# A hybrid decoder block on one core: fewer rotary temporaries, another order of the second block's projections, and a rearranged opening

## The chip, the cores and the metric

The kernel runs on one core of a Trainium2 chip, in one launch. The metric is the device time of that core in microseconds (us), the median of several runs. TensorE (PE in the profile) does the matrix products, VectorE (DVE), ScalarE (ACT) and GpSimd (POOL) the rest, and SyncE (SP) issues nearly all transfers.

## The reference

One layer of a decoder block, float32, 2048 tokens of width 1024 (`x`, one sequence), with a conditioning vector `c`:

```python
mod = c @ w_ada + b_ada
shift_m, scale_m, gate_m, shift_f, scale_f, gate_f = jnp.split(mod, 6, axis=-1)
h = rms_norm(x, g_pre_mix) * (1 + scale_m) + shift_m
q_a, k_a, v_a, q_m, k_m, v_m, o_m, i_m, f_m, g_a, g_m = jnp.split(h @ w_in, split_points, axis=-1)
q_a, k_a = rope(q_a, positions), rope(k_a, positions)      # 8 and 2 heads of 64
y_a = sliding_window_attention(q_a, k_a, v_a, attn_sinks)  # window 128, blocks of 128
qk_m = silu(causal_depthwise_conv([q_m, k_m], conv_w, conv_b))
y_m = sigmoid(o_m) * head_layer_norm(mlstm_chunkwise(q_m, k_m, v_m, i_m + b_i, f_m + b_f), mlstm_norm_w)
merged = sigmoid(g_a) * (y_a @ w_branch_attn) + sigmoid(g_m) * (y_m @ w_branch_mlstm)
x = x + gate_m * rms_norm(merged @ w_out, g_post_mix)
h2 = rms_norm(x, g_pre_ffn) * (1 + scale_f) + shift_f
x = x + gate_f * rms_norm((silu(h2 @ w_ffn_gate) * (h2 @ w_ffn_up)) @ w_ffn_down, g_post_ffn)
```

The mLSTM is a recurrence over time with 4 heads of 128, computed in chunks. `w_ada` is 1024 x 6144, `w_in` 1024 x 4872.

## The kernel before

**Products.** Every large product is done as three TensorE products of rounded high and low parts (`hi`, `lo`, in a 32-bit type for TensorE): for weights ACT makes `whi` (L256, L259) and DVE `wlo` (L257, L260); L204 is the line of all products, L209 that of all transposes. A group of products on one weight slice for four token tiles of 128 fills four PSUM banks, the accumulators `acc`; four more banks (`mix`) serve transposes, attention, the mLSTM and other small products.

**Stages.** The tokens are four blocks of 512, b0 to b3, and two superblocks of two blocks each. The stages with their times in the profile:

- The opening (0 to 66 us). Shift and scale are computed from `w_ada` in four chunks of 256 columns (`ADA`, `ada_first`): the 8 row groups of a chunk are multiplied by the matching element of `c` and summed on DVE (L426, L428), then columns are summed by a product with ones. The shift of the first chunk goes over TensorE: 8 products with `c` as the stationary operand, a copy of the row by ACT (L443), and products that turn it into columns. L448 to L450 make shift and scale columns of it. Between the chunks `hprep` makes the normalized, shifted and scaled, transposed h of b0: squares by ACT (L500), root on POOL (L475), scaling (L506), transposes, high part by ACT (L518), the full value by ACT (L520), low part (L521) by POOL for the first block and by DVE for the others. The products of q for b0 follow the two feature tiles of each chunk as they come.
- Projections of the first block of the superblock (b0, from 66 us; b2, from 750 us): q, kv (k, v and the mLSTM's i and f), vm (the mLSTM's v); then of the second block: vm, q, kv, to about 240 and 960 us. Attention of the first block runs between the second block's products.
- Fourteen pairs, each a product for both blocks of the superblock at once, in seven products instead of eight: mLSTM q and k (`qk`), o (`om`), the two gates (`ga`, `gm`). The mLSTM's chunks run beside them. Then the branch products and `w_out` for each block (`outputs`). To about 750 and 1300 us.
- The FFN (1300 us to the end).

**Rotary tiles.** A tile of q (128 tokens x 512) or k leaves its accumulator by an ACT copy into a buffer `raw` of the pool `tx` (L781 for q, L805 for kv). `rope` takes two more, `y` and `z`: y gets raw times cosine (L758), z the crossed products with sine (L759, L760), L761 and L762 put them together in y. Later, `q_stream` transposes y on TensorE and takes two more `tx` for the high and low parts, which SP stores to `at_d` (L773); `k_stream` takes one more. vm's tiles take one `tx` each (L827) and are stored. The pool `tx` has 9 buffers of 128 x 512; a buffer that is stored is free when its store has landed. `tx` also serves the weights of `ada_stream`, the running computation of the other shift, scale and gate columns, and temporaries of the pairs.

**Order.** The program is written as a list of pieces of TensorE work (`program`, `superblock`); generators (`spawn`) with due times in estimated nanoseconds of TensorE work put their next step between the pieces (`tick`), and `finish` runs a generator to its end. A scheduler then orders each engine's instructions by a model of the times; each engine works off its own queue in order. SP's queue holds nearly all transfers in the order in which they are issued, and a transfer that is issued waits for the landing of one issued some transfers before.

**mLSTM.** In `chunk_state` (L1001), for a chunk of 128 tokens and four heads, the decay weights are exp(min(nb + cl, cneg)): four DVE instructions of 128 x 128 (L1022) and one exp of 128 x 512 (L1023); 16 chunks.

Of the kernel before, what the change touches and what calls it, by code (L numbers as in the profile page):

```python
# [49 lines left out]
ADA = [(0, 256, (0,)), (256, 256, ()), (512, 256, ()), (768, 256, ())]  # L50
# [21 lines left out]
def decoder_block(ctx: ExitStack, tc: tile.TileContext, a: dict, out: bass.AP, dbg=None):  # L72
# [76 lines left out]
    posi = tm([S // P, P], I32)  # L149
    nc.sync.dma_start(posi, a["positions"].rearrange("o (t p) -> (o t) p", p=P))  # L150
    c_sb = const.tile([P, KD], F32, name="c_sb")
    nc.sync.dma_start(c_sb, a["c"].rearrange("o (p k) -> (o p) k", k=KD))
# [3 lines left out]
    nc.sync.dma_start(sinks, a["attn_sinks"].to_broadcast([P, HQ]))  # L156
    ada_raws = {c0: load_ada(c0, n) for c0, n, _ in ADA[:ADA_AHEAD[0]]}
# [272 lines left out]
    def ada_first(c0, n, raws, on_pe):  # L430

        t0, nt = c0 // P, n // P
        acc = [tm([P, n]) for _ in range(2)]
        pt = mix_tile()
        ps = {part: mix_tile() for part in on_pe}
        for k in range(KD):
            for part in (0, 1):
                if part in on_pe:
                    mm(ps[part][0:1, :n], c_sb[:, k:k + 1], raws[part][k], k == 0, k == KD - 1)
                else:  # L440
                    ada_terms(acc[part], raws[part][k].unsqueeze(1), k, 1)
        for part in on_pe:
            A.copy(acc[part][0:1, :], ps[part][0:1, :n])  # L443
        for part in (0, 1):
            r = 1 if part in on_pe else P
            for j in range(nt):
                mm(pt[:, part * 8 + j:part * 8 + j + 1], acc[part][:r, j * P:(j + 1) * P], ones[:r, 0:1], True, True)
        V.tensor_tensor(sh1[:, t0:t0 + nt], pt[:, :nt], col("b_ada", t0, nt), op=ALU.add)  # L448
        V.tensor_tensor(s1[:, t0:t0 + nt], pt[:, 8:8 + nt], b1[:, 8 + t0:8 + t0 + nt], op=ALU.add)
        V.tensor_tensor(s1[:, t0:t0 + nt], s1[:, t0:t0 + nt], col("g_pre_mix", t0, nt), op=ALU.mult)  # L450
# [35 lines left out]
    def hprep(b, first=False):  # L486
# [25 lines left out]
        def one(k):  # L512
# [8 lines left out]
            (G if first else V).tensor_tensor(lo, v, hi.bitcast(F32), op=ALU.subtract)  # L521
# [192 lines left out]

    hp0 = hprep(0, first=True)
    next(hp0)
    tables = {}
# [18 lines left out]
    def superblock(sb):  # L736
# [9 lines left out]
        def rope(raw, heads, b, t):  # L746
# [7 lines left out]
            y = tx([P, W])  # L754
# [1112 lines left out]
```

## Time and profile before

| | us |
|---|---|
| median of 3 runs | 2722.19 (2721.7 to 2723.53) |
| profiled execution | 2727.14 |
| its span | 2725.4 |
| TensorE busy | 2644.5 (97%) |
| DVE busy | 1999.1 (73%) |
| ACT busy | 1287.0 (47%) |
| POOL busy | 152.6 (6%) |

The profile is of one execution, 4.95 us above the median of the runs; 1.7 us lie outside its span. In its rows L12 is line 12 of the kernel, `out<-in` are the program's names with the buffer numbers left out, a number in square brackets is the idle time of the engine just before, with what ended it. A row of a group gives the count, then the total busy time in us, the mean ns of one, and the idle time before them. The clock (PEclk) is that granted to TensorE as a share of the full one. Shares of busy time are means over stages that differ; the windows by stage are read for what one stage is worth.

### The profile page before, as it was taken

How to read it: one execution, taken by the hardware profiler on the slowest of the kernel's cores; microseconds unless marked ns; L12 is line 12 of the kernel's file. 1: busy time of each engine (PE TensorE's matmuls, PEld its weight loads, DVE VectorE, ACT ScalarE, POOL GpSimd, SP SyncE). 2: the span in 40 equal slices, each digit the busy share in tenths (PEclk: the TensorE clock that was granted, in tenths of full speed). 3: DMA queues.
4: the chain of work that ended last, by engine and by line, in shares of the span. 5: the costliest groups of instructions: out<-in, count | busy, mean ns of one | idle time of the engine just before them, and what ended most of it. 6: DMA issues, size and time to landing. Idle time of an engine off the chain costs nothing.

```text
span 2725.4 us, 35775 instructions
## 1 busy us (share of the span) xinstructions
PE 2644.5 (97%) x12310; PEld 2136.0 (78%) x12310; DVE 1999.1 (73%) x3954; ACT 1287.0 (47%) x2510; POOL 152.6 (6%) x189
## 2 busy tenths in 40 slices
PE   6999999999989899999999999999999999999998
PEld 4767778888877677888887888888877888888886
DVE  7959877866786988876587777776677676766456
ACT  5555743444755564334563443335554333333444
POOL 2010101100101010110000000000000000000000
PEclk8999999999999999999999999999999999999999
DMA  7755445697675554568765664436675332324566
GB/s 248 234 154 179 147 136 168 206 333 255 219 231 187 177 160 153 180 218 315 255 198 199 198 192 155 147 121 213 204 272 194 102 115 86 112 93 147 185 210 216
DMA packets 353639, 511.89 MB, mean 188 GB/s; under 512 B 25121, under 2 KB 213661, under 8 KB 348209
## 3 DMA queue, kind: packets, MB, share of 16 engines
q1 hardware_dynamic: 353456, 509.61, 56.6%
q8 instruction: 97, 1.59, 0.2%
q14 instruction: 86, 0.70, 0.1%
HBM read 357.12 MB, written 144.02 MB: 184 GB/s over the span
## 4 chain that ended last, share of the span: by engine, by line
PE 77%; DVE 7%; issue 4%; DMA 2%; ACT 2%; POOL 0%; SPq 0%; DVEq 0%; POOLq 0%; ACTq 0%
PE acc L204 54%; PE mix L204 22%; DVE hl L1354 1%; PE mix L209 1%; ACT hl L1353 1%; DMA at_d<-tx 1%; DMA raw<-as_d 1%; DVE tx L1132 1%; DMA raw<-in_w_ffn_down_dram 1%; DMA raw<-ws_d 0%; DVE w L1664 0%; DVE big L1354 0%; DVE big L552 0%; POOL rs L475 0%; DMA x1n<-tm 0%
## 5 line engine op out<-in xcount | busy, mean ns | idle before, releaser
L204 PE MATMUL acc<-big,hl 128*128 128x512 f32 x3936 | 947.7, 394 | 13.7 <-ACT tx L805 5.9
L204 PEld LDWEIGHTS acc<-big,hl 128*128 128x128 f32 x3936 | 732.8, 189 | 183.3 <-issue 10.2
L1353 ACT CAST hl<-raw 128x512 fp32r<-128x512 f32 x732 | 439.4, 621 | 500.5 <-PE acc L204 233.0
L1354 DVE TENSOR_TENSOR hl<-raw,hl 128x512 fp32r<-128x512 f32 x732 | 495.8, 694 | 193.6 <-ACT hl L1353 192.6
L204 PE MATMUL acc<-whi,big 128*128 128x512 f32 (+1 forms) x1280 | 380.8, 378 | 19.0 <-ACT big L518 8.4
L204 PEld LDWEIGHTS acc<-whi,big 128*128 128x128 f32 x1280 | 236.4, 192 | 65.9 <-ACT big L518 8.5
L204 PE MATMUL mix<-big,hl 128*128 128x512 f32 x1056 | 263.9, 390 | 1.6 <-ACT hl L1353 1.0
L204 PE MATMUL acc<-wlo,big 128*128 128x512 f32 (+1 forms) x640 | 241.8, 380 | 3.4 <-DVE wlo L260 3.4
L204 PE MATMUL acc<-hl,hl 128*128 128x512 f32 x1008 | 237.0, 393 | 4.7 <-DVE hl L1354 2.9
L204 PEld LDWEIGHTS mix<-big,hl 128*128 128x128 f32 x1056 | 197.7, 188 | 46.0 <-DVE hl L1354 1.8
L204 PEld LDWEIGHTS acc<-hl,hl 128*128 128x128 f32 x1008 | 187.1, 188 | 49.8 <-DVE hl L1354 8.4
L204 PE MATMUL mix<-hl,hl 128*128 128x512 f32 x792 | 183.2, 391 | 2.3 <-ACT hl L1353 1.4
L204 PEld LDWEIGHTS mix<-hl,hl 128*128 128x128 f32 x792 | 147.7, 188 | 37.0 <-DVE hl L1354 3.3
L260 DVE TENSOR_TENSOR wlo<-raw,whi 128x1024 fp32r<-128x1024 f32 (+1 forms) x96 | 108.8, 1133 | 71.8 <-ACT whi L259 65.1
L259 ACT CAST whi<-raw 128x1024 fp32r<-128x1024 f32 (+1 forms) x96 | 94.5, 985 | 128.6 <-PE acc L204 123.2
L204 PE MATMUL acc<-big,whi 128*128 128x512 f32 x512 | 154.9, 391 | 0.0
L204 PEld LDWEIGHTS acc<-wlo,big 128*128 128x128 f32 x640 | 123.1, 192 | 29.6 <-DVE wlo L260 5.1
L475 POOL TENSOR_TENSOR rs<-ms,nhalf 128x1 f32<-128x1 f32 (+1 forms) x56 | 42.7, 774 | 1642.4 <-DVE ms L473 1639.7
L204 PE MATMUL mix<-hcT4h,hl 128*128 128x512 f32 x352 | 117.6, 394 | 0.7 <-ACT hl L1353 0.7
L204 PE MATMUL acc<-hcT2h,hl 128*128 128x512 f32 x352 | 117.5, 394 | 0.0
L204 PEld LDWEIGHTS acc<-big,whi 128*128 128x128 f32 x512 | 95.7, 188 | 19.6
L204 PE MATMUL acc<-big,wlo 128*128 128x512 f32 x256 | 96.3, 392 | 0.0
(331 smaller groups left out, 3482.3 us busy)
## 6 DMA issues: line engine op xcount, KB each, us to landing
raw<-in_w_in_dram SPq DMA_DIRECT2D x48, 1024.0 KB
as_d<-w SPq DMA_DIRECT2D x154, 256.0 KB
raw<-as_d SPq DMA_DIRECT2D x70, 512.0 KB
raw<-in_w_ffn_gate_dram SPq DMA_DIRECT2D x22, 1024.0 KB
raw<-in_w_ffn_up_dram SPq DMA_DIRECT2D x22, 1024.0 KB
raw<-ws_d SPq DMA_DIRECT2D x40, 512.0 KB
tx<-in_w_ada_dram SPq DMA_DIRECT2D x64, 256.0 KB
y_d<-tm SPq DMA_DIRECT2D x64, 256.0 KB
```

The costliest lines, as they stand in the source:

```text
L204: T.matmul(o, lhsT=lhsT, rhs=rhs, start=start, stop=stop, skip_group_check=resumed)
L209: T.transpose(o, i, ident[:k, :k])
L259: A.copy(hv, src)
L260: V.tensor_tensor(lv, src, hv.bitcast(F32), op=ALU.subtract)
L475: G.tensor_tensor(r[:, :n], ms[:, :n], nhalf[:, :n], op=ALU.pow)
L1132: V.scalar_tensor_tensor(ac, u[:, j:j + TB], col("conv_w", j * 8 + f), ac, op0=ALU.mult, op1=ALU.add)
L1353: A.copy(v(hi), src)
L1354: V.tensor_tensor(v(lo), src, v(hi).bitcast(F32), op=ALU.subtract)
```

## The change

1. Loads of the opening: x's first half and positions, `c`, the first chunk of `w_ada`, then x's second half; eight loads of small vectors are issued by ScalarE's queue instead of SP's.
2. Shift and scale of the first chunk and the shift of the second go over TensorE, now with a 128 x 128 piece of `w_ada` as the stationary operand and a column of `c` as the moving one, so that the result is a column: 48 products of one column in place of 8 products of 256 and the products that turned rows into columns; the ACT copy goes, and 16 DVE terms. Scale is finished by one DVE instruction a column instead of two for both.
3. The first block's low parts (L521, eight of them) go from POOL to DVE, and the first superblock's rotary tables are emitted ahead of the chunks instead of ahead of the fourth.
4. `rope` works in place in `raw` with one temporary `z`: two `tx` a tile. `q_stream` puts its high part into z and its low part into raw; `k_stream` puts its parts into z.
5. The second block of a superblock is projected in the order kv, q, vm instead of vm, q, kv.
6. The mixer's gate (`ada_stream`) starts at the fifth pair of the first superblock instead of behind b0's kv, with 6000 instead of 5000 ns between its steps. The first eight pairs are in another order; the last `qk` pair takes the place of the second `ga` pair ahead of the point at which the mLSTM starts.
7. `chunk_state` adds nb and cneg in one DVE instruction and leaves cl to the bias of four exps of 128 x 128.

The instructions that TensorE issues from the FFN's first products on keep their order.

```diff
-ADA = [(0, 256, (0,)), (256, 256, ()), (512, 256, ()), (768, 256, ())]
+ADA = [(0, 256, (0, 1)), (256, 256, (0,)), (512, 256, ()), (768, 256, ())]
...
-    x_first = [load_x(x_d, big, 0)]
-
     stack = tm([P, P])
     V.memset(stack, 0.0)
+    posi = tm([S // P, P], I32)
+    nc.sync.dma_start(posi, a["positions"].rearrange("o (t p) -> (o t) p", p=P))
+    x_first = [load_x(x_d, big, 0)]
+    c_sb = const.tile([P, KD], F32, name="c_sb")
+    nc.sync.dma_start(c_sb, a["c"].rearrange("o (p k) -> (o p) k", k=KD))
+    ada_raws = {c0: load_ada(c0, n) for c0, n, _ in ADA[:ADA_AHEAD[0]]}
+    x_first.append(load_x(x_d, big, 1))
...
-        nc.sync.dma_start(stack[r0:r0 + n, :], v)
+        nc.scalar.dma_start(stack[r0:r0 + n, :], v)
...
-    x_first.append(load_x(x_d, big, 1))
...
-    nc.sync.dma_start(b_if, a["b_if"].to_broadcast([P, 8]))
+    nc.scalar.dma_start(b_if, a["b_if"].to_broadcast([P, 8]))
...
-    ada_raws = {c0: load_ada(c0, n) for c0, n, _ in ADA[:ADA_AHEAD[0]]}
...
-        acc = [tm([P, n]) for _ in range(2)]
-        pt = mix_tile()
-        ps = {part: mix_tile() for part in on_pe}
+        acc = {part: tm([P, n]) for part in (0, 1) if part not in on_pe}
+        pt = mix_tile() if acc else None
+        cols_ = {(part, j): (mix_tile if acc else acc_tile)()[:, :1] for part in on_pe for j in range(nt)}
         for k in range(KD):
             for part in (0, 1):
                 if part in on_pe:
-                    mm(ps[part][0:1, :n], c_sb[:, k:k + 1], raws[part][k], k == 0, k == KD - 1)
+                    for j in range(nt):
+                        mm(cols_[part, j], raws[part][k][:, j * P:(j + 1) * P], c_sb[:, k:k + 1], k == 0, k == KD - 1)
                 else:
                     ada_terms(acc[part], raws[part][k].unsqueeze(1), k, 1)
-        for part in on_pe:
-            A.copy(acc[part][0:1, :], ps[part][0:1, :n])
...
-        V.tensor_tensor(s1[:, t0:t0 + nt], pt[:, 8:8 + nt], b1[:, 8 + t0:8 + t0 + nt], op=ALU.add)
-        V.tensor_tensor(s1[:, t0:t0 + nt], s1[:, t0:t0 + nt], col("g_pre_mix", t0, nt), op=ALU.mult)
+        for j in range(nt):
+            t = t0 + j
+            V.tensor_tensor(sh1[:, t:t + 1], cols_[0, j], col("b_ada", t), op=ALU.add)
+            V.scalar_tensor_tensor(s1[:, t:t + 1], cols_[1, j], b1[:, 8 + t:9 + t], col("g_pre_mix", t), op0=ALU.add, op1=ALU.mult)
...
-            (G if first else V).tensor_tensor(lo, v, hi.bitcast(F32), op=ALU.subtract)
+            V.tensor_tensor(lo, v, hi.bitcast(F32), op=ALU.subtract)
...
     hp0 = hprep(0, first=True)
     next(hp0)
-    tables = {}
+
+    tables[0] = rope_tables(0)
...
-            y = tx([P, W])
-            z = tx([P, W])
...
-            return y
+            z = tx([P, 512])
...
+            V.tensor_tensor(zz[:, :, 0, :], src[:, :, 1, :], sb_, op=ALU.mult)
+            V.tensor_tensor(zz[:, :, 1, :], src[:, :, 0, :], sb_, op=ALU.mult)
+            V.tensor_tensor(rr, rr, cb, op=ALU.mult)
+            V.tensor_tensor(src[:, :, 0, :], src[:, :, 0, :], zz[:, :, 0, :], op=ALU.subtract)
+            V.tensor_tensor(src[:, :, 1, :], src[:, :, 1, :], zz[:, :, 1, :], op=ALU.add)
+            return raw, z
...
-            hi, lo = tx([P, 512], F32R), tx([P, 512], F32R)
+            hi, lo = z.bitcast(F32R), y.bitcast(F32R)
...
-            kk = tx([P, 2, P], F32R)
+            kk = z[:, P:3 * P].bitcast(F32R).rearrange("p (i k) -> p i k", i=2)
...
-            V.scalar_tensor_tensor(wd[:, hh, :], nb[:, hh, :], cl[:, t, 0, hh:hh + 1], cneg, op0=ALU.add, op1=ALU.min)
-            A.activation(wd, wd, AF.Exp)
+            V.tensor_tensor(wd, nb, cneg.unsqueeze(1).to_broadcast([P, MH, P]), op=ALU.add)
+            for hh in range(MH):
+                A.activation(wd[:, hh, :], wd[:, hh, :], AF.Exp, bias=cl[:, t, 0, hh:hh + 1])
...
-        if sb == 0:
-            yield lambda: R.update(ada_m=[spawn(ada_stream([(2, "gate")], 5000.0))])
         yield from vm(b0)
...
+        q1, kv1 = (list(z) for z in q_kv(b1))
+        yield from kv1
+        yield from q1
         yield from vm(b1)
-        yield from q_kv(b1)
...
-        pairs = [("qk", 0), ("om", 0), ("qk", 1), ("om", 1), ("qk", 2), ("ga", 0), ("qk", 3), ("ga", 1),
+        pairs = [("om", 0), ("qk", 0), ("om", 1), ("qk", 1), ("ga", 0), ("qk", 2), ("ga", 1), ("qk", 3),
                  ("ga", 2), ("ga", 3), ("gm", 0), ("gm", 1), ("gm", 2), ("gm", 3)]
         for i, (kind, p) in enumerate(pairs):
             parts = list(in_pair(kind, p))
+            if sb == 0 and i == 4:
+                yield lambda: R.update(ada_m=[spawn(ada_stream([(2, "gate")], 6000.0))])
...
-            if (kind, p) == ("ga", 1):
+            if (kind, p) == ("qk", 3):
                 yield lambda: finish(convs + R["gs", b0] + R["gs", b1])
                 yield lambda: spawn(mlstm(), L_ML)
```

More of the change, by code (lines that the diff above doesn't have):

```diff
@@ L1281, in superblock @@
         yield start
-        yield from q_kv(b0)
+        for z in q_kv(b0):
+            yield from z
         yield lambda: attend(b0)
-        if sb == 0:
-            yield lambda: R.update(ada_m=[spawn(ada_stream([(2, "gate")], 5000.0))])
         yield from vm(b0)
```

32 lines of the change are left out of this document (12 added, 20 removed).

## The prediction

> **What bounds the kernel now.** I read the page first, its table of busy time (share of the span, instructions).
>
> ```profile
> span 2725.4 us, 35775 instructions
> PE 2644.5 (97%) x12310; PEld 2136.0 (78%) x12310; DVE 1999.1 (73%) x3954; ACT 1287.0 (47%) x2510; POOL 152.6 (6%) x189
> ```
>
> TensorE is busy for 2644.5 of 2725.4 us, so all that a change of order can win is the 80.9 us in which it is idle, and what a lower clock costs. The table of windows says where that lies; I cut it at the borders of the stages. (Columns: window and its length, then PE, weight loads, DVE, ACT, POOL busy, clock, DMA share, GB/s.)
>
> ```profile
> 0.00:26.10 26.10, 8.19 (x34) 3.90 (x34) 15.72 (x58) 13.96 (x28) 3.97 (x45) 0.97 0.88 309
> 26.10:65.70 39.60, 33.12 (x144) 27.20 (x145) 32.29 (x80) 20.46 (x41) 12.23 (x9) 0.81 0.63 224
> 65.70:110.00 44.30, 40.73 (x242) 35.90 (x241) 40.44 (x106) 26.29 (x44) 1.17 (x2) 0.96 0.56 184
> 110.00:160.00 50.00, 46.41 (x216) 34.75 (x215) 33.31 (x76) 27.58 (x74) 4.16 (x4) 0.93 0.76 243
> 160.00:200.00 40.00, 36.30 (x194) 23.53 (x193) 22.87 (x56) 17.26 (x57) 4.85 (x5) 1.00 0.46 133
> 200.00:240.00 40.00, 32.14 (x158) 25.32 (x158) 35.72 (x101) 18.25 (x39) 0.00 (x0) 0.87 0.72 242
> 240.00:750.00 510.00, 509.30 (x2454) 414.70 (x2453) 393.55 (x855) 269.35 (x531) 52.98 (x51) 1.00 0.61 202
> 750.00:850.00 100.00, 93.13 (x501) 75.71 (x500) 77.63 (x189) 57.30 (x124) 4.22 (x4) 0.98 0.69 220
> 850.00:960.00 110.00, 100.09 (x538) 74.69 (x537) 97.25 (x248) 65.56 (x173) 10.64 (x9) 1.00 0.53 176
> 960.00:1300.00 340.00, 339.46 (x1658) 274.89 (x1657) 266.88 (x583) 155.86 (x290) 34.50 (x28) 1.00 0.62 203
> 1300.00:2725.40 1425.40, 1405.66 (x6184) 1145.41 (x6183) 983.39 (x1608) 615.14 (x1115) 23.86 (x32) 1.00 0.52 173
> ```
>
> The idle time is the length less PE's: 24.4 us in the opening (the first two windows), 7.2 from 65.7 to 160 (b0's kv and vm), 11.6 from 160 to 240 (b1's vm, q, kv), 16.8 from 750 to 960 (the same in the second superblock), 1.2 in the two long stretches of pairs, mLSTM and outputs, 19.7 in the FFN and at the end. The clock adds: 40 us at a mean of 0.87 lose 5.2 us, the 50 us at 0.93 lose 3.5, the 44.3 at 0.96 lose 1.8, the 100 at 0.98 lose 2.0; a part of it falls into idle time. The change touches nothing past 1300 us: what TensorE issues there keeps its order. So its field is the opening, and the 35.6 us of idle time and 12.5 us of lost clock between 65.7 and 960.
>
> What TensorE waits for there, from the table of waits (total us, times, longest) and the timeline (start, length, what, idle time before it):
>
> ```profile
> PE acc L204 <- ACT tx L805: 8.7, 5, 4.3
> PE acc L204 <- ACT tx L781: 4.0, 3, 2.2
> PE acc L204 <- ACT tx L827: 3.8, 3, 2.0
> PE acc L204 <- ACT big L518: 8.4, 2, 4.6
> PE acc L204 <- DVE wlo L260: 3.4, 2, 2.2
> 214.16 8.30 PE L204 MATMUL acc<-big,hl 128*128 128x512 f32 x24 [4.28 <-ACT tx L805]
> 762.82 0.39 PE L204 MATMUL acc<-whi,big 128*128 128x264 f32 x1 [2.15 <-ACT tx L781]
> 788.19 0.50 PE L204 MATMUL acc<-whi,big 128*128 128x512 f32 x1 [1.98 <-ACT tx L805]
> L805 ACT COPY tx<-acc 128x264 f32<-128x264 f32 x16 | 6.0, 385 | 20.3 <-DMA at_d<-tx 11.5 <-DVE tx L760 3.2 <-DVE raw L1446 2.7
> ```
>
> 16.5 us are waits for the evacuations of q (L781), kv (L805) and vm (L827): the accumulator's bank is not free, because ACT's copy has no `tx` buffer to go to. The last row says who holds them: ACT's kv copies stood idle 11.5 us for stores `at_d<-tx`, i.e. for buffers that q and k tiles keep until their stores have landed.
>
> **Part 1, the opening.** The stalls are these, with the rows that time its loads and its DVE work:
>
> ```profile
> 26.14 0.80 PE L204 MATMUL acc<-whi,big 128*128 128x512 f32 x1 [3.79 <-ACT big L518]
> 42.63 0.80 PE L204 MATMUL acc<-whi,big 128*128 128x512 f32 x1 [4.59 <-ACT big L518]
> 41.56 0.15 DVE L450 TENSOR_TENSOR s<-s,cols 128x2 f32<-128x2 f32 x1
> 7.58 3.09 SPq L129 DMA_DIRECT2D big<-in_w_ada_dram  x4
> 11.00:24.00 13.00, 7.46 (x32) 3.54 (x32) 9.53 (x31) 6.95 (x11) 1.29 (x2) 1.00 1.06 380
> L428 DVE SCALAR_TENSOR_TENSOR tm<-big,c_sb,tm 128x256 f32<-128x256 f32 x49 | 25.5, 556 | 0.0
> L521 DVE TENSOR_TENSOR big<-big,big 128x512 fp32r<-128x512 f32 x24 | 16.4, 685 | 8.3 <-ACT big L520 5.9 <-DMA x1n<-tm 2.1
> 8.62 0.63 ACT L500 ACTIVATE big<-big 128x512 f32<-128x512 f32 x1 [0.24 <-DMA big<-in_x_dram]
> 17.89 2.19 ACT L506 ACTIVATE big<-big,rs 128x1024 f32<-128x1024 f32 x2 [4.19 <-POOL rs L475]
> L204 PE MATMUL mix<-ones,tm 128*128 128x1 f32 x60 | 8.5, 250 | 1.9 <-DVE tm L428 1.7 <-ACT cos L679 0.2
> ```
>
> The first chunk's ada weights (2 MB) are issued at 7.58 now, behind ten small loads and both halves of x; after, they go ahead of x's second half (1 MB, landed now when ACT squares it at 8.62). At 380 GB/s those 3 MB take 7.9 us, so that the weights land some 3 us sooner, but x's second half about 7 us later, near 15.6. From there four squares (4 x 0.63), the scaling (2.19), about 1.2 of rs, the transposes and the first h bring me to a first product at about 24.1 instead of 26.14. The second chunk is bound by DVE, which ends its scale at 41.7. DVE loses 16 of its 64 chunk terms; starts follow at 0.4 us (L428 shows 25.5 us for 49 that overlap, records of 0.556), so 6.3 us. It takes over eight subtractions L521 (0.685 each, paced at 0.6: 4.8) and the rotary tables come earlier in its queue. So chunk 1 is ready near 39.9, chunk 2 5 us sooner than now, the last chunk 0.7 sooner, and the q group, which ends at 65.7 now, ends near 63: **-2.7 us**. Bounds: x's late second half costs up to +1 if the casts of the first weights get ahead of the squares in ACT; -6 if DVE's load alone counts. The 34 TensorE instructions more (columns of one element, at most 0.25 each by the last row) take 8.5 us at most and fall in 24.4 us of idle time; without that cover they would cost just that. The six vectors issued by ACT cost nothing: ACT stands idle then, and waits for x (0.24 and more).
>
> **Part 2, two `tx` a rotary tile.** Four q tiles need 8 of 9 buffers instead of 12. In b0 (65.7 to 160) of 7.2 us idle only some is of this sort; a 2.2 us wait for the low weights (wlo L260), and the attention's own, stay. I take **-2.0**, between -1 and -6. In superblock 1, b2 loses the 2.15 at 762.82 with its echo; the kv and vm waits (1.98 each) need the stores to land and stay for the most part: **-2.5**, between -0.5 and -5.
>
> **Part 3, b1 and b3: kv, q, vm.** Now kv's evacuations come last, and behind them at once the first pair waits for accumulators (4.28 at 214.16, and a clock of 0.87 after it). After, kv's tiles find free buffers and the last group is vm, whose copies need one `tx` each and no rotation. Of 16.8 us (11.6 idle, 5.2 clock) between 160 and 240 I take **-10**, between -4 and -14: about 2.5 are the attention's waits for POOL and ACT, which stay. In b3, 9.9 us idle from 850 to 960: **-4.5**, between -1 and -8, as about half is the attention and the first product qk.
>
> **A stall that comes.** In the changed order b1's k transposes stand in TensorE's queue only behind the attention of the tiles 2 and 3, at the start of vm, so k tiles keep their two buffers for a whole group and q's copies wait. Before has no such wait; below it is nothing, above it is the 4.28 of 214.16 in each of b1 and b3. I take **+4** for both, nearer the middle, since a group of TensorE work between lets most of the stores land.
>
> **Part 4, what I cost at nothing.** The gate's `ada_stream` goes into the pairs, om before qk, the mLSTM starts about 25 us of TensorE work later (what stands ahead of its first product in the two orders, summed), and `chunk_state` trades DVE for ACT:
>
> ```profile
> L1022 DVE SCALAR_TENSOR_TENSOR tm<-tm,cl,cneg 128x128 f32<-128x128 f32 x64 | 22.3, 407 | 0.4 <-DMA tm<-negm_d 0.4
> L1023 ACT ACTIVATE tm<-tm 128x512 f32<-128x512 f32 x16 | 10.3, 641 | 4.2 <-DVE tm L1022 4.0
> L428 DVE SCALAR_TENSOR_TENSOR tm<-tx,c_sb,tm 128x512 f32<-128x512 f32 x56 | 43.3, 773 | 5.3 <-DMA tx<-in_w_ada_dram 5.0
> 568.81 1.28 SPq L1094 DMA_DIRECT2D y_d<-tm  x1
> 615.10 1.03 SPq L1177 DMA_DIRECT2D big<-y_d  x2
> ```
>
> DVE saves 4 x 0.35 (the rows overlap, so 0.35 of 0.407) less one add of 0.68 (as L521's) per chunk, 11 us over 16; ACT gains four small exps (estimated at 0.3 each) for one of 0.64, some 9 us. The gate's 16 terms are 12.4 us of DVE. All of it lies under TensorE, busy 509.3 of 510 and 339.5 of 340 us there, with DVE at 77% and ACT at 53%. If the cover were gone (the last mLSTM chunk late for the outputs), it would cost what the 25 us exceed the slack: the last store of an mLSTM chunk (L1094) is issued at 568.81, its load (L1177) at 615.10, so 46 us are there and 21 would be left.
>
> **Sum**: -2.7 -2.0 -2.5 -10 -4.5 +4 = -17.7. Against the profiled execution, 2727.14 us (span 2725.4 and 1.7 outside it), that is 2709.4; that run lies 4.95 above the median of the runs, 2722.19, so by ratio (0.9935) the forecast is **2704.5 us**.
>
> **The clock's share.** A short stall costs more than itself here:
>
> ```profile
> 129.04 0.97 PE L204 MATMUL mix<-at 64*128 64x256 f32 x6 [1.39 <-ACT tm L931]
> 130.20:137.00 6.80, 6.80 (x19) 4.96 (x19) 6.80 (x14) 2.15 (x6) 0.00 (x0) 0.50 0.61 162
> 789.00:792.40 3.40, 3.40 (x10) 2.66 (x9) 3.02 (x9) 1.04 (x1) 0.00 (x0) 0.50 0.42 149
> ```
>
> Gaps of 1.39 and 1.98 us are followed by 6.8 and 3.4 us at half clock, PE busy throughout: 3.4 and 1.7 us lost. Of my sum about 5.5 us are such losses (4 in b1, 1.5 elsewhere). The Trainium skill's page "TensorE: Matmul & The Clock Gate" (Part 1, the HAM clock gate, and "HAM oscillation") puts the fall to half rate behind an idle window of about 3.4 us. By that rule gaps under it would cost only themselves; the two rows speak against it here, as both gaps are shorter.
>
> **Rivals.**
> - *All goes*: the stalls vanish with their echoes and nothing new comes: 6 in the opening, 6, 5, 14 and 8 of the upper bounds, less some overlap, -33: 2689. For it: 16.5 us of the waits name the same buffers. Against: kv and vm still wait for landings.
> - *Stalls move*: a tile is freed only when its store lands, in place of when DVE is through, so what is won in b0 to b3 comes back at the next copy. Only the opening counts: about 2719.5, no change. For it: the 11.5 us that L805 waited for stores.
> - *Slower by k's tiles*: k's transposes, late in TensorE's order, hold two `tx` each, and q's copies stop the accumulators in all four blocks. The price is the largest such stall, 4.28 and half of 6.8 us of half clock, 7.7 a block: +31 less 18 of gains, 2735. It decides once q's copies lag over a group of products (some 22 us for four tiles). Against: b0 and b2 keep their order.
> - *The short-gap rule* holds for the gaps that go (their half clock has another cause and stays): 5.5 less gained, 2710.
> - *The opening doesn't gain*: x's second half is late; 2707, inside the forecast's own range.
>
> **How the numbers follow.** The forecast has 0.55, all goes 0.15, stalls move 0.11, slower 0.14, the clock rule 0.05. The range takes in the terms' bounds and *stalls move*, and stops short of *slower* and of the outer part of *all goes*: 2687 to 2722. 0.2% is 5.4 us, about what can be told from no change: faster is below 2716.7. *Stalls move* splits 2 to 9 between faster and same: faster 0.77, same 0.09, slower 0.14.
>
> **What would show it.** Right: the wait for L781 gone from the table, L805 under 4 us, PE's idle time from 160 to 240 under 5 us with a clock near 1.0, the q group ending near 63, all starts past 1300 us shifted alike. Wrong: new waits for L781 with releaser `at_d<-tx` or the k copies; PE idle in 240 to 750; a first product later than 26.

## The result, and the profile after

The changed kernel takes **2715.3 us** (median of 8 runs, 2709.65 to 2718.78) against 2722.78 us for the kernel before (8 runs, 2721.47 to 2726.76): ratio 0.9969 with a 95% interval of 0.9958 to 0.998. That is 7.5 us less; 2704.5, 18 us less, had been forecast. Its profiled execution took 2712.38 us, of which the span is 2710.5.

In the changed kernel's rows most lines are shifted by one or two: L203 are the products, L208 the transposes, L782 q's, L807 kv's and L828 vm's evacuation, L951 is L950 of before. Its page and its waits:

```profile
span 2710.5 us, 35922 instructions
PE 2648.8 (98%) x12378; PEld 2156.8 (80%) x12378; DVE 1980.8 (73%) x3902; ACT 1300.5 (48%) x2557; POOL 135.3 (5%) x181
PE acc L203 <- DMA big<-in_w_ada_dram: 9.5, 1, 9.5
PE mix L208 <- POOL tm L951: 8.7, 7, 3.5
PE acc L203 <- ACT tx L828: 4.2, 3, 1.4
PE mix L208 <- DVE tm L864: 3.9, 1, 3.9
PE acc L203 <- ACT tx L782: 0.8, 1, 0.8
PE acc L203 <- ACT tx L807: 0.3, 1, 0.3
```

TensorE's idle time fell from 80.9 to 61.7 us. But 13.6 of these 19.2 us lie in the opening (24.4 idle before, 10.8 now, by the first two windows), and the opening is hardly shorter for it: TensorE does more small products there. The waits for q's and kv's copies, 12.7 us before, are down to 1.1, as forecast; 4.2 for vm's copies are left (3.8 before). In their place stand waits of the attention, 8.7 for POOL (L951, the softmax's division; 2.8 before), and of the mLSTM's gates, 3.9 for L864.

The windows at the same borders as before (columns as there):

```profile
0.00:26.10 26.10, 16.28 (x75) 15.51 (x76) 8.43 (x36) 12.85 (x25) 3.94 (x45) 1.00 0.85 303
26.10:65.70 39.60, 38.62 (x180) 32.90 (x179) 34.66 (x99) 21.72 (x43) 1.33 (x2) 1.00 0.66 228
65.70:110.00 44.30, 41.62 (x254) 36.22 (x255) 40.50 (x108) 28.59 (x49) 0.54 (x2) 1.00 0.60 193
110.00:160.00 50.00, 42.93 (x231) 33.27 (x229) 33.39 (x113) 25.11 (x73) 4.32 (x4) 0.90 0.56 177
160.00:200.00 40.00, 37.54 (x199) 26.97 (x199) 28.76 (x67) 23.42 (x66) 4.68 (x5) 1.00 0.52 150
200.00:240.00 40.00, 39.90 (x207) 31.86 (x206) 31.81 (x77) 25.79 (x74) 2.95 (x3) 1.00 0.55 203
750.00:850.00 100.00, 89.86 (x528) 73.88 (x528) 78.35 (x230) 56.72 (x135) 4.73 (x5) 0.95 0.68 221
850.00:960.00 110.00, 103.49 (x497) 75.08 (x498) 89.99 (x199) 63.80 (x159) 8.50 (x9) 0.95 0.55 176
```

Between 160 and 240 idle time fell from 11.6 to 2.6 us, and the clock's dip there is gone. But 110 to 160 has 7.1 idle instead of 3.6, and superblock 1 (750 to 960) 16.7 instead of 16.8, with a clock of 0.95 where it was 0.98 and 1.00. All that was forecast for superblock 1 is missing.

### The profile page after: what moved, and what is told of

It reads as the page before. It is cut to its first block, busy times and chain, and to the rows that moved or that the text cites. A ratio compares the mean times of both kernels' runs of the same rounds, so it can differ in the third digit from the quotient of the medians.

```text
span 2710.5 us, 35922 instructions
## 1 busy us (share of the span) xinstructions
PE 2648.8 (98%) x12378; PEld 2156.8 (80%) x12378; DVE 1980.8 (73%) x3902; ACT 1300.5 (48%) x2557; POOL 135.3 (5%) x181
## 4 chain that ended last, share of the span: by engine, by line
PE 82%; DVE 8%; DMA 5%; ACT 4%; issue 1%; POOL 0%; SPq 0%; DVEq 0%; POOLq 0%; ACTq 0%
PE acc L203 58%; PE mix L203 22%; PE mix L208 2%; DVE hl L1358 1%; ACT hl L1357 1%; DMA raw<-as_d 1%; ACT tm L947 1%; DMA big<-big 1%; DMA raw<-ws_d 1%; DVE tm L427 1%; DMA big<-in_x_dram 1%; DMA raw<-in_w_ffn_down_dram 1%; DVE wlo L259 0%; ACT big L499 0%; DVE big L551 0%
## 5 line engine op out<-in xcount | busy, mean ns | idle before, releaser
L203 PE MATMUL acc<-big,hl 128*128 128x512 f32 x3936 | 939.8, 393 | 4.7 <-ACT tx L828 2.7
L203 PEld LDWEIGHTS acc<-big,hl 128*128 128x128 f32 x3936 | 733.3, 188 | 172.0 <-issue 10.6
L203 PE MATMUL acc<-whi,big 128*128 128x512 f32 (+1 forms) x1280 | 380.2, 377 | 2.8 <-ACT tx L828 1.4
L203 PEld LDWEIGHTS acc<-whi,big 128*128 128x128 f32 x1280 | 235.6, 191 | 45.8 <-ACT tx L828 1.6
L203 PE MATMUL mix<-big,hl 128*128 128x512 f32 x1056 | 263.9, 391 | 1.9 <-ACT hl L1357 1.2
L203 PE MATMUL acc<-wlo,big 128*128 128x512 f32 (+1 forms) x640 | 240.5, 378 | 3.1 <-DVE wlo L259 3.0
L203 PE MATMUL acc<-hl,hl 128*128 128x512 f32 x1008 | 237.2, 393 | 5.9 <-DVE hl L1358 3.4
L203 PEld LDWEIGHTS mix<-big,hl 128*128 128x128 f32 x1056 | 197.9, 188 | 45.9 <-ACT hl L1357 2.0
L203 PEld LDWEIGHTS acc<-hl,hl 128*128 128x128 f32 x1008 | 187.1, 188 | 51.3 <-DVE hl L1358 9.0
L203 PE MATMUL mix<-hl,hl 128*128 128x512 f32 x792 | 183.1, 392 | 1.8 <-DVE ms L472 0.9
L203 PEld LDWEIGHTS mix<-hl,hl 128*128 128x128 f32 x792 | 147.8, 188 | 36.4 <-ACT hl L1357 3.0
L203 PE MATMUL acc<-big,whi 128*128 128x512 f32 x512 | 157.5, 393 | 0.0
L203 PEld LDWEIGHTS acc<-wlo,big 128*128 128x128 f32 x640 | 122.5, 191 | 25.8 <-DVE wlo L259 5.1
L203 PE MATMUL mix<-hcT4h,hl 128*128 128x512 f32 x352 | 117.7, 395 | 0.7 <-ACT hl L1357 0.7
L203 PE MATMUL acc<-hcT2h,hl 128*128 128x512 f32 x352 | 117.6, 395 | 0.0
L203 PEld LDWEIGHTS acc<-big,whi 128*128 128x128 f32 x512 | 95.4, 188 | 19.2
L203 PE MATMUL acc<-big,wlo 128*128 128x512 f32 x256 | 97.6, 393 | 0.0
```

The lines of the kernel that those rows point to most:

```text
L203: T.matmul(o, lhsT=lhsT, rhs=rhs, start=start, stop=stop, skip_group_check=resumed)
```

## The experiments

**The yardstick: both kernels again.** The first profile of before was a long execution, 2727.14 us against a median of 2722.8. Both kernels were profiled and timed a second time, unedited.

> The kernel before again, unedited, for a second profile. The first profiled execution took 2727.1 us against a median of 2723.5, the changed kernel's 2712.4 and 2713.6 against 2715.2, so the two profiles differ by 14.8 us and the medians by 8. Theory A (the first profile was a long execution of before, by stalls that other executions don't have): the second lies near 2723, and the stage that is shorter shows which 3 to 4 us of the profile's 14.8 are not the change's. Theory B (profiled executions of before are always longer): 2727 again, the stages alike within 0.5 us.

> The changed kernel again, unedited, for the spread of its profile and times. Theory A (the same work gives the same stalls, and executions differ by the places where the clock falls): median 2713 to 2717 us, the stalls of the projections at the same places within 0.5 us, the windows of half clock at others. Theory B (the stalls themselves differ from run to run, by transfers that land at other times): stalls of 1 us and more at other instructions.

Measured: before 2722.69 (ratio to the other runs of before 1.0002, 0.9993 to 1.0011), changed 2715.14 (0.9965, 0.9953 to 0.9978). The windows below are cut at each execution's own stages, before_again first: projections of superblock 0 (first kv product to first pair's product), pairs and b0's branch products to the first product of b0 with `w_out`, from there to superblock 1's first pair, from there to the first product of b2 with `w_out` (the expectations say "up to the FFN" for this border).

```profile
66.30:209.20 142.90, 128.44 (x710) 99.55 (x708) 108.93 (x260) 79.30 (x190) 9.59 (x11) 0.99 0.64 206
209.20:593.70 384.50, 380.38 (x1855) 305.45 (x1856) 311.85 (x730) 186.58 (x380) 36.71 (x30) 1.00 0.58 188
593.70:889.50 295.80, 285.82 (x1446) 230.83 (x1444) 215.33 (x468) 175.82 (x369) 25.78 (x30) 0.99 0.68 228
889.50:1280.00 390.50, 383.19 (x1872) 307.01 (x1873) 324.11 (x747) 187.60 (x381) 39.33 (x32) 1.00 0.60 195
```

```profile
65.80:208.70 142.90, 130.67 (x720) 102.28 (x720) 110.90 (x303) 81.80 (x197) 9.63 (x11) 0.96 0.59 187
208.70:583.10 374.40, 374.30 (x1844) 304.32 (x1843) 298.96 (x658) 189.81 (x398) 34.07 (x30) 1.00 0.61 194
583.10:889.80 306.70, 292.80 (x1462) 237.71 (x1460) 227.68 (x529) 178.77 (x375) 25.41 (x30) 0.96 0.68 231
889.80:1269.90 380.10, 377.06 (x1857) 305.63 (x1858) 309.05 (x668) 192.33 (x401) 37.68 (x32) 1.00 0.61 196
```

Theory A holds for before: in the first profile the first stretch took 147.8 us (66.35 to 214.16, by the same borders), here 142.9. The difference is for the most part the 1.39 us gap at 129.04 and the half clock behind it, which I had quoted as a typical row; the second execution doesn't have it. For the changed kernel A holds mostly: the 3.54 us wait for L951 and those of 1.2 to 2.0 us near it come back at the same instructions. Against before_again, superblock 0 is, in these single executions, 10.1 us shorter (517.3 against 527.4) and superblock 1 0.5 longer (686.8 against 686.3).

**One part at a time, on the kernel before.** Each is the part of the same number in the list of the change, alone; for the gate, of part 6, only its stream:

```diff
# e1: parts 1 to 3 (opening)      # e2: part 4 (two tx a tile)      # e3: part 5, below
+        q1, kv1 = (list(z) for z in q_kv(b1))
+        yield from kv1
+        yield from q1
         yield from vm(b1)
-        yield from q_kv(b1)
# e16: the gate's stream
-        if sb == 0:
-            yield lambda: R.update(ada_m=[spawn(ada_stream([(2, "gate")], 5000.0))])
...
+            if sb == 0 and i == 4:
+                yield lambda: R.update(ada_m=[spawn(ada_stream([(2, "gate")], 6000.0))])
```

> The kernel before with the rearranged opening alone (loads, first chunk and second shift over TensorE, low parts on DVE, rotary tables earlier); all later code is that of before. Theory A (the opening gives next to nothing: in the changed kernel the q group of b0 ended at 65.0 us against 65.7, since TensorE's idle time turned into slower and more small products): -1 us, between -3 and +1; the q group ends near 65. Theory B (the opening gives the forecast's 2.7 us and the rest of the change takes it back): -3 to -5 us.

> The kernel before with two temporaries a rotary tile alone. Theory A (the waits for L781, L805 and L827 are of the buffers' number, and two temporaries take most of them away): PE's idle time in the projections of both superblocks falls by some 10 us, the time by 6 to 10 us. Theory B (a tile is freed only when its store lands, so the stalls move): the waits for L805 and L827 stay at 8 to 12 us in sum, the time within 3 us of before.

> The kernel before with the second block of a superblock projected as kv, q, vm alone, three temporaries as before. Theory A (the order wins the stall of 4.3 us ahead of the first pair of superblock 0 with its half clock, and loses it again in superblock 1, where the first block's attention stands exposed: in the changed kernel the stretch from 583 to 888 us lost 8.6 us against before): first pair of superblock 0 some 5 us sooner, that of superblock 1 with nothing left of it; time -3 to +3 us. Theory B (the order is the gain, in both superblocks): -8 to -12 us. Theory C (with three temporaries the order is worse, since four q tiles of b1 follow kv's tiles at once): +5 us or more.

> The kernel before with the gate's stream moved to the fifth pair at 6000 ns, and nothing else. Within the change, this move is worth 13.1 us. Theory A (it is a gain of its own: the weights' tx buffer and the DVE terms are taken out of the projections): 5 to 12 us faster than before, 2711 to 2718, with the wait for L805 ahead of the first pair under 2 us. Theory B (it gains only together with two temporaries and the new order, since with three temporaries the buffers are short anyway): within 3 us of before.

| on before, alone | median us | before, same runs | ratio (95%) |
|---|---|---|---|
| e1 opening | 2727.05 | 2723.46 | 1.0010 (1.0001 to 1.0019) |
| e2 two temporaries | 2728.82 | 2723.46 | 1.0021 (1.0012 to 1.0030) |
| e3 order kv, q, vm | 2732.76 | 2723.46 | 1.0031 (1.0019 to 1.0044) |
| e16 gate's stream | 2713.79 | 2722.82 | 0.9968 (0.9956 to 0.9981) |

The three parts that I had counted as gains lose when alone. Neither theory of e1 nor of e2 gave a loss that large, and e3 is its theory C. The part that I had costed at nothing gains 9 us, more than the whole change; theory A of e16 had that, though not that a wait of 3.5 us for L805 would be left ahead of the first pair.

**Parts taken out of the changed kernel, or put together.**

```diff
# e6: before + parts 4 and 5        # e7: changed - part 6      # e8: changed - parts 1 to 3
# e9: changed, the gate's stream back behind b0's kv            # e10: changed, the pairs' order back
# e11: changed - part 7             # e13: changed - part 5     # e14: changed - part 4
# e12: changed, part 5 in superblock 0 alone (e15: the same, and - parts 1 to 3)
-        q1, kv1 = (list(z) for z in q_kv(b1))
-        yield from kv1
-        yield from q1
-        yield from vm(b1)
+        if sb == 0:
+            q1, kv1 = (list(z) for z in q_kv(b1))
+            yield from kv1
+            yield from q1
+            yield from vm(b1)
+        else:
+            yield from vm(b1)
+            for z in q_kv(b1):
+                yield from z
# e18: changed - parts 1 to 3 - part 5
```

> The kernel before with two temporaries a rotary tile and the second block projected as kv, q, vm, together; alone they measured 5.4 and 9.3 us slower. Theory A (they need each other: with two temporaries a tile the order's kv and q tiles fit into the nine buffers): superblock 0's projections and pairs together near the 517.5 us of the changed kernel (before 533.2), time 4 to 10 us under before. Theory B (what each costs adds up): +10 to +15 us.

> The changed kernel with the order of the pairs and the place and spacing of the gate's stream as before. Theory A (they are off the path): within 2 us of the changed kernel, 2713 to 2717. Theory B (the gate's weights hold a tx buffer and DVE in the second block's projections): 4 to 8 us slower than the changed kernel, with stalls for tx between 110 and 210 us.

> The changed kernel with the opening as before. Alone the new opening measured 3.6 us slower than before. Theory A (it is a loss also within the change): 2 to 4 us faster than the changed kernel, near 2712. Theory B (within the change, it is a gain of 1 to 3 us): 2716 to 2718.

> The changed kernel with only the gate's stream put back behind b0's kv, at 5000 ns; the pairs keep their new order. With both put back it measured 2731.6 against 2715.2. Theory A (the gate's weights take a tx buffer while the rotary tiles of b0 and b1 need eight of nine, so the copies of vm and q wait): most of the 16 us comes back, 2727 to 2732, with waits for L828 and L782 of 8 us and more in sum between 110 and 215 us. Theory B (the order of the pairs is what counts): within 4 us of the changed kernel.

> The changed kernel with only the order of the first eight pairs put back; the gate's stream stays at the fifth pair. Theory A (the gate's place counts): within 4 us of the changed kernel, 2712 to 2719. Theory B (the order of the pairs counts, as om first gives the stalled qk time): 2723 or more, the loss in the pairs' stretch of superblock 0.

> The changed kernel with the decay weights of the mLSTM chunks made as before (four DVE instructions and one exp). Theory A (hidden under TensorE): within 2 us of the changed kernel. Theory B (DVE's saving shortens the chain of a chunk, on which the pairs and outputs wait): 3 us slower or more.

> The changed kernel with the new order of the second block in superblock 0 alone; b3 is projected as vm, q, kv as before. Theory A (in superblock 1 the order only moves stalls, from the first pair to b3's kv and q beside b2's attention): 2712 to 2717, the stretch of superblock 1 up to the FFN within 3 us of 686.4. Theory B (in superblock 1 the order costs, and two temporaries would gain alone): 4 to 8 us faster than the changed kernel. Theory C (the order gains there and something else takes it back): 4 us slower or more.

> The changed kernel with the second block projected as vm, q, kv as before, in both superblocks. With the new order in superblock 0 alone it measured 2709.8, with both 2715.2. Theory A (the order gains in superblock 0 what the prediction gave it, 10 us, and costs 5.4 in superblock 1): 2718 to 2721. Theory B (the gains of superblock 0 are the two temporaries' and the gate's place; the order gains nothing there either): 2708 to 2712.

> The changed kernel with three temporaries a rotary tile. On the kernel before, the new order cost 9.3 us with three and gained 4.2 with two temporaries. Theory A (the order needs the two temporaries): 10 to 16 us slower than the changed kernel, 2725 to 2731, with waits for L782 or L807 and L828 of 10 us and more. Theory B (with the gate's stream out of the way nine buffers do for three temporaries too): within 4 us of the changed kernel.

> The changed kernel with the new order in superblock 0 alone and the opening as before: both edits that measured as losses taken out. If they add up, 2709.8 - 1.6 = 2708, between 2706 and 2711; if they don't, 2710 to 2713.

> The kernel before with the two temporaries, the gate's move, the pairs' order and the new decay weights; the opening and the order of the second block as before. Within the change, taking out the order gave 10.8 us and taking out the opening 1.6 (4.3 to 6.3 where the order is back in superblock 1). If they add up: 2698 to 2703; if the opening's loss needs the new order: 2703 to 2706.

| kernel | median us | ratio to before (95%) | against the changed kernel's 2715.2 |
|---|---|---|---|
| e6 temporaries and order, on before | 2717.99 | 0.9986 (0.9977 to 0.9995) | |
| e7 pairs and gate back | 2731.55 | 1.0033 (1.0021 to 1.0045) | +16.3 |
| e8 opening back | 2713.59 | 0.9965 (0.9953 to 0.9976) | -1.6 |
| e9 gate back | 2728.27 | 1.0023 (1.0014 to 1.0032) | +13.1 |
| e10 order of pairs back | 2717.35 | 0.9973 (0.9963 to 0.9983) | +2.1 |
| e11 decay weights back | 2715.51 | 0.9970 (0.9959 to 0.9981) | +0.3 |
| e12 order in superblock 0 alone | 2709.75 | 0.9949 (0.9936 to 0.9961) | -5.4 |
| e13 order back in both | 2704.37 | 0.9931 (0.9919 to 0.9944) | -10.8 |
| e14 three temporaries back | 2719.83 | 0.9988 (0.9979 to 0.9997) | +4.6 |
| e15 as e12, opening back | 2703.49 | 0.9927 (0.9915 to 0.9939) | -11.7 |
| e18 opening and order back | **2702.79** | 0.9918 (0.9905 to 0.9932) | -12.4 |

e8, e10 and e11 can't be told from the changed kernel (their intervals overlap its own; theory A for e10 and e11, neither for e8). e9 is its theory A and puts the worth of part 6 on the gate's stream: superblock 0's projections take 154.5 us there against 142.9, and TensorE waits 12.4 us in them for vm's and q's copies (8.6 for L828, 3.8 for L782). e7 is theory B in kind, at twice its size. e12 is theory B, and e13 goes beyond it: the order costs in superblock 0 too. e14 lies near theory B, e15 below both its theories. In e6 the time is theory A's, but superblock 0 took 524.9 us and not 517.5. e18 is the sum that was expected. Together they give a path on which each step is one measured kernel: before 2722.8; the gate's move, 2713.8 (-9.0); two temporaries, with the pairs' order and the decay weights, 2702.8 (-11.0); the new order of the second block, 2713.6 (+10.8, e18 to e8); the opening, 2715.2 (+1.6). These are differences of medians taken at different times, and before itself measured 2722.2 to 2723.9 beside them; with each kernel set against the before of its own runs, the steps are -9.0, -12.1, +12.5 and about +1.

```profile
66.20:220.70 154.50, 129.04 (x716) 100.51 (x716) 119.07 (x311) 81.58 (x195) 9.52 (x11) 0.98 0.63 203
```

The row is e9's first stretch. The order's sign changes with what stands around it: with the stream behind b0's kv the new order takes the kernel with two temporaries from 2728.8 to 2718.0 (e2 to e6); with the stream in the pairs it costs as much, some 10 to 12 us (e18 to e8), about half of it in each superblock (e13, e12, changed). That it is the gate's place which turns the sign is concluded from e9 (13.1 us) and e10 (2.1 us); the two comparisons also differ in the pairs' order and the decay weights, and no run changes the gate's place alone between them.

**What the gate's stream did in the projections.** Timeline of before_again, the buffers first (SP's loads of g's row for L419 and of the second half's weights), then the product that L419 waits for, the DVE instructions and the store that free the buffers, then the copies of b1's four q tiles, the transposes of the first and a step of the second one's rotation:

```profile
126.98 0.36 SPq L417 DMA_DIRECT2D tx<-in_g_post_mix_dram  x1
129.51 0.35 SPq L459 DMA_DIRECT2D tx<-in_w_ada_dram  x1
139.54 2.31 SPq L459 DMA_DIRECT2D tx<-in_w_ada_dram  x4
187.48 1.12 PE L204 MATMUL mix<-tm,ones 128*128 128x512 f32 x2
188.65 0.69 DVE L419 TENSOR_TENSOR tx<-mix,tx 128x512 f32<-128x512 f32 x1 [0.72 <-PE mix L204]
189.37 0.33 SPq L420 DMA_DIRECT2D gg_m_d<-tx  x1
192.54 0.48 DVE L426 TENSOR_SCALAR tm<-tx,c_sb 128x512 f32<-128x512 f32 x1
170.83 0.59 ACT L781 COPY tx<-acc 128x512 f32<-128x512 f32 x1 [0.96 <-PE acc L204]
174.50 0.57 ACT L781 COPY tx<-acc 128x512 f32<-128x512 f32 x1
191.73 0.59 ACT L781 COPY tx<-acc 128x512 f32<-128x512 f32 x1
194.57 0.59 ACT L781 COPY tx<-acc 128x512 f32<-128x512 f32 x1 [2.25 <-PE mix L209]
189.55 0.66 PE L209 MATMUL mix<-ident,tx 128*128 128x128 f32 x4
190.24 0.42 DVE L759 TENSOR_TENSOR tx<-tx,sin 128x256 f32<-128x256 f32 x1 [0.91 <-PE mix L209]
```

The stream holds not one buffer but six of nine: five with the second half's weights from 129.5 and 139.5 on, whose first term (L426) runs at 192.54, and the one of L419, which waits to 188.65 for a product that comes in TensorE's queue at 187.48. Two q tiles get a copy. The other three buffers are then taken by the first tile's y and the second tile's raw and y, and the second tile's rotation breaks off: its cosine product runs at 175.11, its first sine product, which needs a z, only at 190.24. In the trace it waits for the transposes of the first tile's y at 189.55, which free that buffer. The third copy follows at 191.73, and the third tile's y then waits for the landing of the store of 189.37. ACT and TensorE worked on the attention meanwhile; how much of the 15 us is the shortage, and how much the order that the scheduler gave the queues, is not shown apart. With the stream in the pairs (e16) the four copies begin within 7.3 us (the first and the last are shown), and the stretch to the first pair is 10.1 us shorter than 142.9:

```profile
169.55 0.59 ACT L781 COPY tx<-acc 128x512 f32<-128x512 f32 x1 [0.96 <-PE acc L204]
176.80 0.59 ACT L781 COPY tx<-acc 128x512 f32<-128x512 f32 x1
66.50:199.30 132.80, 123.13 (x709) 96.14 (x707) 100.80 (x246) 79.27 (x190) 9.81 (x11) 1.00 0.60 192
```

Of these 10.1 us, 4.8 are idle time of TensorE (14.5 to 9.7) and 1.7 a stretch of half clock at 79.6 us that only before_again has; the rest is busy time of the same products and isn't taken apart. e16's profiled execution is 3.9 us above its median: from b0's first `w_out` product to b2's it took 692.3 us against 686.3, which is open too.

One run was to tell a buffer from DVE's and the loads' time:

```diff
+    def hold_stream(gap):                      # e17, spawned at the gate's old place, on e16
+        acc = const.tile([P, 4], F32, name="hold_acc")
+        V.memset(acc, 0.0)
+        for ch in range(2):
+            for k in range(KD + 1):
+                raw = tx([P, 1, 512])
+                nc.sync.dma_start(raw[:, 0, 0:4], w_ada[:, ch * 512:ch * 512 + 4]...[:, k % KD, :])
+                yield gap
+                V.tensor_tensor(acc, acc, raw[:, 0, 0:4], op=ALU.add)
```

> The kernel with the gate's stream alone moved to the fifth pair (2713.8), and a stand-in put at its old place: it takes a tx buffer for as long, step by step, with a load of 4 columns in place of 512 and a DVE add of 128 x 4 in place of the 0.77 us terms; it adds a sum that nothing uses. Theory A (what the gate's stream costs in the projections is the ninth tx buffer): 2719 to 2724, back at before, with q's copies for b1 (L781) waiting again near 175 to 195 us. Theory B (it is its 12.4 us of DVE and 4 MB of loads): 2712 to 2716.

Measured 2717.34 us (ratio 0.9977, 0.9968 to 0.9986), between the two, with an interval that overlaps e16's, and the stretch itself stayed short:

```profile
66.80:200.60 133.80, 125.66 (x709) 99.24 (x707) 102.42 (x262) 79.13 (x190) 9.45 (x11) 0.97 0.59 188
```

133.8 us, so a buffer taken step by step costs that stage 1 us. But the stand-in has no tail: it lacks L419 and its product, behind which the real stream's weights waited, and the `tm` buffer that the sums hold until then. So it speaks against the cost of a single buffer and doesn't try the six; that these are the cause is read from the timeline, not shown by a run. A rival is left untested: every edit makes the scheduler order all queues anew, and no run keeps the order and changes the buffers alone. Where the other 2.5 us of e17 are is open.

**What the new order costs.** Superblock 1, from b0's first `w_out` product to b2's, e12 with the old order there:

```profile
582.60:879.20 296.60, 286.85 (x1446) 230.82 (x1444) 216.98 (x474) 177.15 (x370) 25.89 (x30) 1.00 0.69 234
879.20:1266.20 387.00, 381.96 (x1872) 307.75 (x1873) 318.19 (x721) 192.54 (x405) 39.23 (x32) 1.00 0.61 196
```

683.6 us against the changed kernel's 686.8: with the new order the stretch to the first pair is 10.1 us longer (306.7 against 296.6), and the pairs win 6.9 of it back (380.1 against 387.0). The clock in the first of the two is 1.00 here and 0.96 there. What the changed kernel has in this place and e12 doesn't are these rows of its b2 attention, beside b3's kv and q, and a stretch of half clock (the last row):

```profile
839.80 2.73 PE L203 MATMUL mix<-at 64*128 64x256 f32 x24 [2.02 <-DMA at<-at_d]
843.73 3.50 PE L203 MATMUL mix<-at 64*128 64x256 f32 x24 [1.20 <-DVE tm L934]
850.76 1.11 PE L208 MATMUL mix<-ident,tm 128*128 128x128 f32 x4 [3.54 <-POOL tm L951]
840.10:857.20 17.10, 11.89 (x64) 8.05 (x60) 8.36 (x26) 11.31 (x45) 2.96 (x3) 0.50 0.25 81
```

There are 6.8 us of waits in 13 us of time, for a load, for DVE, and for the softmax chain that ends on POOL, and TensorE has half its clock for 17.1 us. Superblock 0 shows the same shape. e13, with the old order in both, takes 135.5 us to the first pair where the changed kernel takes 142.9, and 379.8 behind it where that takes 374.4:

```profile
66.30:201.80 135.50, 127.71 (x706) 99.62 (x707) 104.52 (x252) 79.57 (x191) 9.93 (x11) 0.96 0.58 184
201.80:581.60 379.80, 379.80 (x1859) 305.18 (x1858) 308.81 (x710) 192.00 (x403) 34.97 (x30) 1.00 0.61 197
```

The profiles so show about 5 of the 10.8 us between the medians; e13's profiled execution was 3.7 us above its median. Why the order brings the attention's steps so close together was not taken apart further.

## Why the prediction was wrong, though its direction held

The parts are numbered here as in the prediction: 1 the opening, 2 the two temporaries, 3 the order of the second block, 4 the rest.

- **Direction and range held, the size didn't**: 7.5 us of 18. That the direction held is luck: the largest gain, 9.0 us alone, is the move of the gate's stream, which the prediction costed at nothing, and the three parts that it counted as gains lose when alone.
- **Part 3 failed, and in sign.** The -10 and -4.5 for the order kv, q, vm were priced from stalls that do go, but they go without the order too: the 4.28 at 214.16, ahead of the first pair, is 3.5 with the gate's stream moved (e16) and gone with two temporaries besides, under the old order (e13, e18). With both in place the order costs 10.8. I had read in the groups that L805 waited 11.5 us for `at_d<-tx` and taken the rotary tiles for the only holders, where the timeline shows six buffers with the gate's stream.
- **Part 4 failed.** For the gate's stream I named the cover at the place where it goes, and left out what it leaves: -9.0 alone, 13.1 within the change. The timeline of before showed it: its loads x4 and, 50 us later, the terms. The other terms of that part held: the decay weights are 0.3 us, the pairs' order 2 us, both within what can be told.
- **Part 2 was mis-sized**: -4.5 forecast; with the gate away two temporaries (with the pairs' order and the decay weights) bring 11, within the change 4.6, and alone they cost 5.4.
- **Part 1 failed.** -2.7 forecast; in every pair of kernels that differ in the opening the new one is slower, by 1.6 (e8), 1.6 (e13 to e18), 3.6 (e1) and 6.3 us (e12 to e15), of which the first two can't be told from nothing. In the stage itself nothing is won: the first kv product begins at 66.3 us in the mean of the ten profiles with the new opening (65.6 to 67.8) and at 66.4 in that of the ten with the old one (66.2 to 66.9). Rows of the changed kernel:

```profile
9.33 1.28 ACT L499 ACT_TABLE_LOAD   x1 [9.33 <-DMA tm<-in_mlstm_norm_w_dram]
10.62 0.63 ACT L499 ACTIVATE big<-big 128x512 f32<-128x512 f32 x1
9.36 0.38 SPq L118 DMA_DIRECT2D big<-in_x_dram  x1
18.73 0.63 ACT L499 ACTIVATE big<-big 128x512 f32<-128x512 f32 x1 [2.06 <-DMA big<-in_x_dram]
26.09 3.41 PE L203 MATMUL mix<-c_sb,big 128*128 128x1 f32 x16
29.36 0.78 PE L203 MATMUL acc<-whi,big 128*128 128x512 f32 x1
```

  The first product came at 29.36 instead of 24.1, for three reasons. x's second half was squared at 18.73 instead of 15.6, after a wait for its load, which SP had issued only at 9.36. The casts of the first weights (2.18 us) stood ahead of the scaling; the prediction had that as a bound of up to +1. And products of one column stood ahead in TensorE's queue from 26.09 on. The prediction counted 34 more of these at 0.25 us each; but each is two instructions in the profile (the page has 68 more), and TensorE's busy time in the opening grew by 13.6 us, not by 8.5 at most. The eight issues by ScalarE (the prediction says six), costed at nothing as it stands idle, held its queue to 9.33, so that x's first squares began at 10.62 instead of 5.82; as ACT then waited for x's second half all the same, this is not what delayed the first product. What made up for all this is a thing I had not counted: TensorE's clock stood at 1.00 through the opening, where it was 0.81. Why the whole loses more than the stage does is open.
- **The stall to come** (+4) did not come where it was put: the waits for q's copies are 0.8 us, those for vm's 4.2, where they were 3.8. Other waits came, and no term of the sum had them: 5.9 more for POOL, and 3.9 for the gates (L864).
- **The base was wrong by some 4 us.** One execution carried a chance stall with its half clock. How much of that is in the terms which were read from it is not known.
- **The clock's share failed.** Some 5.5 us of lost clock were to be won. By the windows at the same borders, 65.7 to 960 us lost 12.5 before and 15.5 after (some 5 in before_again): the dip behind b1's gaps went (0.87 to 1.00 between 200 and 240), and others came from 110 to 160 and in superblock 1. A clear gain, some 8 us, lies in the opening, where it was not counted.
- **The rule for short gaps** that the prediction named as a rival finds no support here. In before the window from 110 to 160 had a mean clock of 0.93 with the gap of 1.39 us; in before_again, without that gap, the same window has 1.00:

```profile
110.00:160.00 50.00, 47.98 (x235) 35.90 (x232) 35.31 (x79) 28.55 (x76) 4.17 (x4) 1.00 0.84 267
```

  So half clock came with a gap far shorter than the idle window of about 3.4 us in "TensorE: Matmul & The Clock Gate" (Part 1, the HAM clock gate) of the Trainium skill. But a gap of that size doesn't always bring it: a wait of 2.24 us ahead of 78.26 us in before_again is followed by 3.4 us at half clock, the same wait (2.23) in e16 is not.

## What to carry to other kernels

When a copy waits for a buffer, list every holder of that pool at that moment from the timeline, with the load that fills it and the instruction that frees it, before giving the stall to the edit at hand. A step that is moved has two prices: what it meets at its new place, and what it gives back at the old one. Parts that pay for the same short pool don't add up: one order was worth some -10 us or some +10, by what else had changed.

## What the runs showed of the hardware

With the products of one column from 9.48 us on TensorE's granted clock stood at 1.00 through the whole opening, against 0.81 from 26 to 66 us before. Eight of the ten profiles with the new opening show this; the other two (e1, e10) have 0.91 and 0.96 from 26 to 66 us, and the ten with the old opening 0.80 to 0.84. That these products keep the clock up is read from the profiles; no run had them alone.

```profile
9.48 8.24 PE L203 MATMUL acc<-c_sb,big 128*128 128x1 f32 x38 [9.48 <-DMA big<-in_w_ada_dram]
```

An issue that waited held the whole queue of its engine here. ScalarE's stood for 5.2 us in its row of eight issues, between the fourth and the fifth: in the trace the fifth waits for the semaphore of SP's load of x's first half, which was full at 7.84. ScalarE's first own work began at 9.33.

```profile
2.33 0.29 ACTq L150 DMA_DIRECT2D tm<-in_g_pre_ffn_dram  x1
7.87 0.32 ACTq L150 DMA_DIRECT2D tm<-in_conv_w_dram  x1
```
